# An order held by hand where attention ends and the output projection begins: weight splits among the last queries' steps, table transposes behind the first products

## The chip, the cores and the metric

The kernel runs on one core of a Trainium2 chip. The metric is device time in microseconds of one execution; the number for a kernel is the median over several executions. Five engines work side by side, each through its own queue in order: TensorE (PE, with PEld for its weight loads), VectorE (DVE), ScalarE (ACT), GpSimd (POOL) and SyncE (SP, which only issues transfers here).

## The reference, cut to what matters

One layer of a hybrid decoder on 512 prompt tokens and 8 sample tokens: two mixers, sparse attention (8 heads) and a gated recurrence (4 heads), then the output projection with a residual, then a routed mixture of 16 experts.

```python
o_nsa, o_hgrn, states = mixer(parts, l)
mixed = jnp.concatenate([rms_norm(o_nsa, g_nsa_out[l]), o_hgrn], axis=-1) @ w_out[l]
x = x + gt_a * rms_norm(mixed, g_post_mix[l])
h = rms_norm(x, g_pre_ffn[l]) * (1.0 + sc_f) + sh_f
ffn = hier_moe(h, ...)      # logits of the router: h @ w_rg, h @ w_re
x = x + gt_f * rms_norm(ffn, g_post_ffn[l])
```

## The kernel before

The program is traced in Python by generators that yield between small steps; strings such as `ORD_E` and `ORD_W` say in which order the steps are traced. A scheduler then writes the queue of each engine. It goes by the traced order among the instructions that it takes to be ready, and by its own estimate of when they are ready; so the order in a queue can differ from the traced one. `tc.issue_after(i)` adds, for each instruction that its block traces on the engine of `i`, that it stands behind `i` in that engine's queue. It adds no wait. From the routing on, the order of four engines is written out by hand; the stretch that the change touches is left to the scheduler.

**The last queries.** `attn(i)` handles 128 queries; `attn(3)` is the last (`gens["d"]`). It has eight steps (two groups of heads, four blocks of keys). A step computes scores on PE (lines 1071 and 1073, into one of two `mm` buffers), four exponentials on ACT (line 1077, into one of three `PT` buffers), and, for the first block of a group, a mask on POOL (line 1079). It then multiplies the weights of the step before by the values on PE (line 1085). After the eighth step come the last values, a square (line 1097), sums (line 1100) and the split of the result into two halves (lines 1107 and 1108). Beside it runs `hgrn_samples` (`h`), the recurrence of the eight samples: updates on DVE (line 1144), products on PE (line 1150), sums on DVE (line 1154), a norm on ACT (lines 1160, 151 and 153), a scaling on DVE (line 1162) and a transpose on PE (line 1165). The prompt's recurrence ends in transposes at line 1041.

**The splits.** A product with float32 weights is made from three products of rounded parts. `split` (lines 113 to 115) writes the high part on ACT (line 114) and the rest on DVE or POOL (line 115). `first_half` (`f`) splits the first four of eight pieces of `w_out`: loaded into `wq0` to `wq3`, high parts in `ewh0` to `ewh3`, rests in `ewr` tiles. Then it splits the four heads `mixT` of the recurrence into `mhh` and `mlh`. These tiles lie in the pool `wpa`, which is opened where the closed pools of the recurrence lay. `ORD_E` traces all four weight splits after the first step of `attn(3)`, ahead of its second.

**The projection.** `wout(hf, t, ...)` makes 24 products (line 1301) for one half of the columns and 128 tokens, first with the recurrence's parts, then with the attention's, and ACT and DVE take the result (lines 1304 and 1305). `wout_samples` does the samples (lines 1314 to 1319). `router_weights` begins by transposing the table `GC` on PE (line 1347, eight of them), and multiplies it by the router's weights (lines 1352 and 1355). `ORD_W` traces `ffhhrl...`: first product group, samples, two splits of the second half, then that part of the router. ACT also issues the transfers of `GA`, `GB` and `GC`, and the zeros for `Y` (line 1257).

Of the kernel before, what the change touches and what calls it, by code (L numbers as in the profile page):

```python
# [4 lines left out]

# [11 lines left out]
AF = mybir.ActivationFunctionType  # L17
ALU = mybir.AluOpType
# [41 lines left out]
ORD_E = "dhfdhfdhfdhfdhdhdhdhdhdhhhh"  # L60
# [6 lines left out]
def body(tc, I, O):  # L67
    nc = tc.nc
    es = ExitStack()
    dve, act, pool, pe, sp = nc.vector, nc.scalar, nc.gpsimd, nc.tensor, nc.sync  # L70
# [40 lines left out]
        return t.rearrange("p (h n) -> p h n", h=2)  # L111

    def split(src, hi, lo, eng=None):
        act.activation(hi, src, AF.Copy)  # L114
        (eng or dve).tensor_tensor(lo, src, hi.bitcast(F32), op=ALU.subtract)  # L115

    def en(i):
        return {"d": dve, "p": pool}[ENG[i]]
# [54 lines left out]
    def play(order, **gens):  # L173

        for c in order:
            next(gens[c], None)
        for g in gens.values():
            for _ in g:
                pass
# [733 lines left out]
    def gated_raw():  # L913

        with tc.issue_after(tails[3][4]):
            act.activation(hk, hl, AF.Sigmoid, scale=-1.0)
            done.append(act.activation(hl, hl, AF.Sigmoid).ins)
        for h in range(4):
            pool.tensor_scalar(hk[:, h], hk[:, h], lbt[:, 5, h:h + 1], None, op0=ALU.mult)
            dve.tensor_scalar(hsn[:, 0, h], hl[:, h, NP:T], lbt[:, 5, h:h + 1], lbt[:, 4, h:h + 1], op0=ALU.mult, op1=ALU.add)  # L920
        yield
        with tc.issue_after(tails[3][4]):
            act.activation(hq, hq, AF.Silu)
            for h in range(4):
                done.append(act.activation(mixT[4 + h], mixT[4 + h], AF.Silu).ins)
        yield
        with ExitStack() as behind:
            for i in done:
                behind.enter_context(tc.issue_after(i))
            table = act.preload_act_table_set("natural_log_exp_and_others").ins  # L930
            behind.enter_context(tc.issue_after(table))
            for h in range(4):
                act.activation(hl[:, h, 0:NP], hl[:, h, 0:NP], AF.Ln, scale=lbt[:, 5, h:h + 1], bias=lbt[:, 4, h:h + 1])
        pool.tensor_copy(hsn[:, 1], hk[:, :, NP:T])
        pool.tensor_copy(hsn[:, 2], hq[:, :, NP:T])
        for h in range(4):
            pool.tensor_copy(hsn[:, 3, h], mixT[4 + h][:, NP:T])
        yield

    def hgrn_values():  # L940
        kvs = [wip.tile([128, T], F32, name="kvt") for h in range(2)]

        def turned_values(h):
            o = kvs[h % 2]
            yield from proj_steps(22 + h, o)
            pt = ps_t()
            for t in range(4):
                pe.transpose(pt[:, 128 * t:128 * t + 128], o[:, 128 * t:128 * t + 128], ident)
            dve.tensor_copy(hv[:, :, 128 * h:128 * h + 128], pt.rearrange("p (t c) -> p t c", t=4))
            pt = ps_t()  # L950
            pe.transpose(pt[0:8, 0:128], o[:, NP:T], ident)
            dve.tensor_copy(hvs[:, 128 * h:128 * h + 128], pt[0:8, 0:128])
            yield

        yield from ahead(turned_values(h) for h in range(4))
# [90 lines left out]
    gens = dict(v=hgrn_values(), g=gated_raw(), **{"4567"[h]: mx4[h] for h in range(4)})  # L1046
# [124 lines left out]
    raw = []  # L1171
# [14 lines left out]
    hs = hgrn_samples()  # L1186
    gens.update(h=hs, o=first_weights(), w=copy_windows(), **{"abcd"[i]: attn(i) for i in range(4)})
    with contextlib.ExitStack() as order:
        if DMAN:
            order.enter_context(tc.manual_schedule(engines={pe.engine}))  # L1190
        for c in ORD_F:
            next(gens[c], None)
        drained({c: gens[c] for c in "abcow4567"})
        s_hm.close()
        s_hg.close()

        wpa = open_pool("wpa", 1, es)
        slot = [lambda dt, c=c: wpa.tile([128, D], dt, name=f"ewr{c}") for c in range(6)]  # L1200
        hslot = [lambda dt, c=c: wpa.tile([128, D], dt, name=f"ewh{c}") for c in range(4)]
        high = [h(F32R) for h in hslot]
        mh2 = [wpa.tile([128, D], F32R, name=f"mhh{c}") for c in range(4)]
        mhh, mlh = ([mh2[2 * q + h // 2][:, 512 * (h % 2):512 * (h % 2) + 512] for h in range(4)] for q in range(2))
        load_wout(slot[2](F32))
        load_wout(slot[3](F32))

        def halves(x):
            return x.rearrange("p (a b) -> p a b", a=2)

        def wout_half(hf, wh, wl):
            for q, kk in enumerate(KKS):
                c = 4 * hf + q
                lo = slot[(4, 5, 0, 1, 8, 9, 2, 3)[c]](F32R)
                split(raw[c], high[c], lo, en(93 + c))
                wh[kk], wl[kk] = halves(high[c]), halves(lo)
                yield

        ws, wt2 = ([None] * 4, [None] * 4), ([None] * 4, [None] * 4)

        def first_half():
            for _ in wout_half(0, *ws):
                pass
            yield
            for h in range(4):
                split(mixT[4 + h][:, 0:NP], mhh[h], mlh[h], en(101 + h))
                yield

        fh = first_half()
        play(ORD_E, h=hs, d=gens["d"], f=fh)  # L1230
    s_at.close()
    s_nb.close()

# [21 lines left out]
    for t in range(5):  # L1255
        n = 128 if t < 4 else 8
# [34 lines left out]
    aft = open_pool("aft", 1, s_af, "right")  # L1291
    rn = aft.tile([128, 4], F32, name="rn")

    def wout(hf, t, wh, wl):
        pm = ps_mm()
        for kk in (2, 3, 0, 1):
            for k2 in range(2):
                k = 2 * (kk % 2) + k2
                a, b = (mhi[k], mlo[k]) if kk < 2 else (mhh[k], mlh[k])
                for j, (a, b) in enumerate(((a, wh), (a, wl), (b, wh))):  # L1300
                    pe.matmul(pm[:, kk // 2], a[:, 128 * t:128 * t + 128], b[kk][:, k2],
                              start=(k == 0 and j == 0), stop=(k == 3 and j == 2))
        m = x1[t][:, 512 * hf:512 * hf + 512]
        act.activation(m, pm[:, 1], AF.Copy)
        dve.scalar_tensor_tensor(m, pm[:, 0], rn[:, t:t + 1], m, op0=ALU.mult, op1=ALU.add)
# [16 lines left out]
    GA, GB, GC = (aft.tile([128, 2, 512], F32, name=f"tab{q}") for q in range(3))  # L1322
# [9 lines left out]
    wrt = aft.tile([128, KT, 32], F32, name="wrt")  # L1332
    act.dma_start(wrt, I["wrt"])
    brt = aft.tile([128, 20], F32, name="brt")
# [5 lines left out]
    cW = aft.tile([128, 2, 20], F32, name="cW")  # L1340

    def router(src, n, w):
        hT = aft.tile([128, KT, 128], F32, name="hT", bufs=2)
        for kk in range(2):
            pt = ps_t()
            for k in range(4):
                pe.transpose(pt[:, 128 * k:128 * k + n], src[:, (4 * kk + k) * 128:(4 * kk + k + 1) * 128], ident[:n, :n])
            evac(hT[:, 4 * kk:4 * kk + 4, 0:n], pt.rearrange("p (k t) -> p k t", k=4)[:, :, 0:n])
        pl = ps_o()
        for r_ in range(2):  # L1350
            for q in range(4):
                pe.matmul(pl[32 * q:32 * q + 32, 0:n], w[:, 4 * r_ + q, :], hT[:, 4 * r_ + q, 0:n], start=(r_ == 0), stop=(r_ == 1))
        lT = aft.tile([128, 128], F32, name="lT", bufs=2)
        dve.tensor_copy(lT[:, 0:n], pl[:, 0:n])
        pe.matmul(pl[0:n, 256:276], lT[:, 0:n], sel20, start=True, stop=True)
        return pl[0:n, 256:276]
# [4 lines left out]
    mixed = {}  # L1361

    def router_weights():
        dve.tensor_tensor(cW[:, 0], router(GC.rearrange("p a b -> p (a b)"), 128, wrt), brt, op=ALU.add)
        yield
        gc = srow(aft, 0, 1, bufs=1)
        dve.tensor_tensor(cW[0:8, 1], router(gc.rearrange("p a b -> p (a b)"), 8, wrt), brt[0:8], op=ALU.add)
        yield
        for kk in range(2):
            pt = ps_t()  # L1370
            for k in range(4):
                pe.transpose(pt[:, 128 * k:128 * k + 128], GB[:, kk, 128 * k:128 * k + 128], ident)
            dve.tensor_copy(bT[:, 4 * kk:4 * kk + 4], pt.rearrange("p (k t) -> p k t", k=4)[:, :, 0])
        dve.tensor_tensor(wrb, wrt, bT.unsqueeze(2).to_broadcast([128, KT, 32]), op=ALU.mult)
# [49 lines left out]
    high = high[4:8] + mh2  # L1424
# [356 lines left out]
    last = {w: u for u, (w, c) in enumerate(units)}  # L1781
# [10 lines left out]
    with tc.manual_schedule(engines=MANUAL and {getattr(nc, e).engine for e in MANUAL}):  # L1792
# [7 lines left out]
        for o in ORD_M:  # L1800
            u = k[o] if o in k else 0
            if o in k:
                k[o] += 1
                w, c = units[min(u, len(units) - 1)]
# [65 lines left out]
    for t in range(5):  # L1870
        n = 128 if t < 4 else 8
# [18 lines left out]
    for t in (4, 0, 1):  # L1890
        n = 128 if t < 4 else 8
# [9 lines left out]
    for t in (4, 0, 1, 2, 3):  # L1901
        n = 128 if t < 4 else 8
# [3 lines left out]
    for t in (4, 0, 1, 2, 3):  # L1906
        y, yg = rows_[t]
        n = y.shape[0]
# [5 lines left out]
    for t in (4, 0, 1, 2, 3):  # L1914
        y, yg = rows_[t]
        n = y.shape[0]
# [138 lines left out]
```

## Time and profile before

| what | us |
|---|---|
| median of 3 runs | 747.39 (746.75 to 752.22) |
| the profiled execution | 741.32 |
| its span | 739.6 |
| TensorE busy in the span | 643.4 |

The page and the views give times within the span, from its start. In a timeline, equal neighbours are merged into one row (x4 is four instructions), so the busy time of a row can hold short waits between them; a bracket tells how long the engine had been idle and who ended it. [...]

### The profile page before, as it was taken

The page shows a single profiled execution, that of the slowest core. Times are in us where ns is not written, and L with a number is a line of the kernel's source. Part 1 is how long each engine was busy: PE and PEld are TensorE (multiplying, and loading weights), DVE is VectorE, ACT ScalarE, POOL GpSimd, SP SyncE. Part 2 cuts the span into 40 slices and gives each one's busy share as a digit, 9 for nine tenths or more (in the row PEclk, how much of TensorE's full clock was granted, in tenths as well). Part 3 has the DMA queues.
Part 4 walks back from the last instruction along what each step waited for, and adds up shares of the span by engine and source line. Part 5 has one row for each costly group of instructions (what it writes and reads, how often), then busy time and mean ns, then how long its engine had stood idle before and what let it go on. Part 6 is the DMA issues. An engine that isn't in the chain of part 4 may idle for free. (4 is left out here: it accounts for less than half of the span.)

```text
span 739.6 us, 13131 instructions
## 1 busy us (share of the span) xinstructions
PE 643.4 (87%) x4510; PEld 480.1 (65%) x4510; DVE 456.3 (62%) x1092; ACT 372.2 (50%) x770; POOL 153.4 (21%) x183
## 2 busy tenths in 40 slices
PE   3886898999899989899999989995889999999940
PEld 1754766779688778799776546573456677666620
DVE  3722623345686875667885254456887966888824
ACT  3322523324554545462554545346475757888833
POOL 1000310001141050150110131634211222222113
PEclk9998999999999999999999999998799999999985
DMA  8887698875554545312632274349899889998526
GB/s 282 278 292 252 219 322 294 309 260 176 184 181 143 174 125 182 118 58 85 265 119 84 92 250 140 120 136 345 279 384 356 260 230 321 346 331 287 156 31 231
DMA packets 74605, 160.83 MB, mean 217 GB/s; under 512 B 11346, under 2 KB 39538, under 8 KB 74146
## 3 DMA queue, kind: packets, MB, share of 16 engines
q1 hardware_dynamic: 59808, 125.98, 49.7%
q10 hardware_dynamic: 10690, 25.39, 10.1%
q0 software_dynamic: 4032, 8.53, 5.3%
q8 instruction: 38, 0.62, 0.4%
q14 instruction: 37, 0.30, 0.1%
HBM read 145.29 MB, written 24.28 MB: 229 GB/s over the span
## 5 line engine op out<-in xcount | busy, mean ns | idle before, releaser
L576 PE MATMUL pp<-hhi,wh 128*128 128x260 f32 x256 | 74.9, 292 | 0.3 <-ACT kvt L454 0.3
L576 PE MATMUL pp<-hlo,wh 128*128 128x260 f32 x256 | 73.1, 286 | 0.0
L576 PE MATMUL pp<-hhi,wl 128*128 128x260 f32 x256 | 72.9, 285 | 0.0
L1720 POOL DMA_INDIRECT Y<-ot,gi x17 | 24.4, 1438 | 129.9 <-ACT ot L1719 122.8
L668 ACT ACTIVATE jn<-P,M 128x128 bf16<-128x128 f32 (+3 forms) x64 | 35.9, 561 | 29.2 <-DVE M L666 24.0
L576 PEld LDWEIGHTS pp<-hhi,wh 128*128 128x128 f32 x256 | 48.2, 188 | 3.1 <-issue 2.4
L576 PEld LDWEIGHTS pp<-hlo,wh 128*128 128x128 f32 x256 | 48.2, 188 | 2.0 <-issue 1.8
L576 PEld LDWEIGHTS pp<-hhi,wl 128*128 128x128 f32 x256 | 48.2, 188 | 1.4 <-issue 1.2
L115 DVE TENSOR_TENSOR wl<-wr,wh 128x1024 fp32r<-128x1024 f32 x9 | 11.3, 1250 | 38.4 <-ACT wh L114 38.4
L1077 ACT ACTIVATE PT<-mm 128x256 f32<-128x256 f32 x80 | 24.3, 389 | 19.8 <-PE mm L1073 19.8
L666 DVE CUSTOM_DVE_ANT_0 P<-mm,tb 128x128 f32<-128x128 f32 (+3 forms) x64 | 29.1, 484 | 5.8 <-PE mm L659 5.8
L410 PE MATMUL mm<-hhi,wh 128*128 128x260 f32 x144 | 30.0, 288 | 1.3 <-ACT wh L114 1.3
L114 ACT ACTIVATE wh<-wr 128x1024 fp32r<-128x1024 f32 x9 | 9.5, 1056 | 41.7 <-PE mm L410 22.1
L410 PE MATMUL mm<-hlo,wh 128*128 128x260 f32 x144 | 30.0, 285 | 0.0
L659 PE MATMUL mm<-ka,qs 128*128 128x512 f32 (+2 forms) x112 | 27.3, 352 | 3.1 <-DVE mx L779 1.7
L1691 PE MATMUL pf<-ewi,xh 128*96 128x512 f32 x72 | 29.8, 413 | 0.0
L410 PE MATMUL mm<-hhi,wl 128*128 128x260 f32 x144 | 29.8, 287 | 0.0
L1691 PE MATMUL pf<-ewi,xl 128*96 128x512 f32 x72 | 28.8, 400 | 0.0
L1718 ACT ACTIVATE ot<-mm 96x512 f32<-96x512 f32 x17 | 10.1, 594 | 33.3 <-PE mm L1715 33.3
L1073 PE MATMUL mm<-qs,ka 128*128 128x512 f32 x80 | 25.6, 399 | 0.0
L410 PEld LDWEIGHTS mm<-hhi,wh 128*128 128x128 f32 x144 | 22.2, 188 | 5.0 <-issue 3.4
L410 PEld LDWEIGHTS mm<-hhi,wl 128*128 128x128 f32 x144 | 22.2, 188 | 3.5 <-issue 3.4
(657 smaller groups left out, 1838.6 us busy)
## 6 DMA issues: line engine op xcount, KB each, us to landing
ewr<-in_ew SPq DMA_DIRECT2D x37, 512.0 KB
wa<-in_wa SPq DMA_DIRECT2D x16, 1024.0 KB
wr<-in_wi ACTq DMA_DIRECT2D x25, 512.0 KB
ewt<-in_ew SPq DMA_DIRECT2D x24, 512.0 KB
cg<-in_cc SPq DMA_DIRECT2D x64, 128.0 KB
ewh<-in_ew SPq DMA_DIRECT2D x16, 512.0 KB
x<-in_ew SPq DMA_DIRECT2D x15, 512.0 KB
mh<-in_wa SPq DMA_DIRECT2D x13, 512.0 KB
```

Source lines behind the costliest of these rows:

```text
L114: act.activation(hi, src, AF.Copy)
L115: (eng or dve).tensor_tensor(lo, src, hi.bitcast(F32), op=ALU.subtract)
L410: pe.matmul(p[:, hf, 0:260], a[:, k, :], b[:, k, hf * 260:hf * 260 + 260], start=(k == 0 and j == 0), stop=(k == KT - 1 and j == 2))
L576: pe.matmul(p[:, 0:260], a[:, k, :], b[:, k, c], start=(k == 0 and j == 0), stop=(k == KT - 1 and j == 2))
L659: pe.matmul(o, QS[g][:, h % 4, qc], KA[g][:, j, a:b], start=(j == 0), stop=(j == 1))
L666: dve.tensor_tensor_reduce(out=p, in0=sb[:, br], in1=tb0[:, 384 - 128 * i:512].rearrange("p (k n) -> p k n", n=128), scale=SL[h], scalar=1 ...
L668: act.activation(jn[:, 0:128 * (i + 1)], p.rearrange("p k n -> p (k n)"), AF.Exp, scale=-1.0, bias=M[:, 0, i, br, h:h + 1], accum_out=M[:, ...
L1073: pe.matmul(S[:, br], KS[g][:, q, br, j], QS[g][:, :, qc], start=False, stop=(q == 1))
L1077: act.activation(PT[:, :, h], S4[:, :, h], AF.Exp, scale=-SL[4 * g + h])
L1691: pe.matmul(pg, a[:, k, :], b[:, wk_], start=(k == 0 and j == 0), stop=(k == 7 and j == 2))
L1718: act.activation(o3[:, 0], pd[:, 0], AF.Copy)
L1720: pool.indirect_dma_start(out=Y, out_offset=bass.IndirectOffsetOnAxis(ap=gix, axis=0), in_=ot, in_offset=None, bounds_check=T - 1, oob_is_ ...
```

## The change

`split` now returns its ACT instruction. `wout_half` collects them in `cuts`. While `attn(3)` is played in the order of `ORD_E`, each of its steps that is traced after the weight splits is put behind one of them in ACT's queue: the step at position 3 behind the second split, all later ones behind the fourth. In the projection, `wout` collects its last PE instruction in `wout_end`, and the PE instructions of the router's first part (eight transposes, sixteen products, two selections) are put behind the last product of the first group. No instruction is added or taken away.

```diff
     def split(src, hi, lo, eng=None):
-        act.activation(hi, src, AF.Copy)
+        cut = act.activation(hi, src, AF.Copy).ins
         (eng or dve).tensor_tensor(lo, src, hi.bitcast(F32), op=ALU.subtract)
+        return cut
...
-                split(raw[c], high[c], lo, en(93 + c))
+                cuts.append(split(raw[c], high[c], lo, en(93 + c)))
...
-        play(ORD_E, h=hs, d=gens["d"], f=fh)
+
+        last = dict(h=hs, d=gens["d"], f=fh)
+        for n, c in enumerate(ORD_E):
+            with tc.issue_after(cuts[1 if n < 6 else 3]) if cuts and c == "d" else nullcontext():
+                next(last[c], None)
+        play("", **last)
...
-                    pe.matmul(pm[:, kk // 2], a[:, 128 * t:128 * t + 128], b[kk][:, k2],
+                    mm = pe.matmul(pm[:, kk // 2], a[:, 128 * t:128 * t + 128], b[kk][:, k2],
                               start=(k == 0 and j == 0), stop=(k == 3 and j == 2))
+        wout_end.append(mm.ins)
...
-        dve.tensor_tensor(cW[:, 0], router(GC.rearrange("p a b -> p (a b)"), 128, wrt), brt, op=ALU.add)
+        with tc.issue_after(wout_end[0]):
+            dve.tensor_tensor(cW[:, 0], router(GC.rearrange("p a b -> p (a b)"), 128, wrt), brt, op=ALU.add)
```

## Rows read from the trace of the kernel before

**Rows 1.** The page's first part: busy time and share of the span of each engine.
```profile
PE 643.4 (87%) x4510; PEld 480.1 (65%) x4510; DVE 456.3 (62%) x1092; ACT 372.2 (50%) x770; POOL 153.4 (21%) x183
```

**Rows 2.** The table of stretches: the last queries, the seam, the projection, the mixture of experts. Columns: stretch, its length, busy us and instructions of PE, PEld, DVE, ACT, POOL, granted clock, DMA share, GB/s.
```profile
411.30:424.30 13.00, 13.00 (x86) 7.88 (x84) 2.18 (x8) 6.03 (x22) 1.09 (x1) 1.00 0.11 42
424.30:434.60 10.30, 7.84 (x36) 3.05 (x33) 6.97 (x9) 7.88 (x16) 5.81 (x6) 0.83 0.58 202
...
452.30:474.50 22.20, 22.18 (x143) 14.01 (x142) 13.14 (x23) 12.75 (x27) 9.37 (x7) 1.00 0.37 125
474.50:504.60 30.10, 28.10 (x166) 20.80 (x167) 13.61 (x27) 11.06 (x28) 12.55 (x8) 0.94 0.48 157
...
535.00:712.00 177.00, 166.11 (x828) 116.66 (x826) 139.78 (x198) 125.82 (x194) 38.97 (x31) 0.99 0.87 283
```

**Rows 3.** The same table, finer, inside the seam.
```profile
426.70:429.10 2.40, 0.00 (x0) 0.00 (x0) 2.40 (x4) 2.40 (x4) 0.31 (x1) 0.97 0.47 142
429.10:432.55 3.45, 3.44 (x5) 0.54 (x5) 2.78 (x4) 3.08 (x10) 3.45 (x3) 0.53 0.95 329
```

**Rows 4.** The timeline of PE from the last queries to the router's first transposes: start, busy us, line, operation, count.
```profile
409.80 0.44 PE L1041 MATMUL pt<-ident,hq 128*128 128x128 f32 x2
...
412.91 1.08 PE L1085 MATMUL po<-PT,VT 128*64 128x256 f32 x8
...
415.52 1.08 PE L1085 MATMUL po<-PT,VT 128*64 128x256 f32 x8
...
419.13 0.64 PE L1150 MATMUL pt<-S,qm 128*32 128x128 f32 x16
...
423.91 1.08 PE L1085 MATMUL po<-PT,VT 128*64 128x256 f32 x8
...
426.02 0.63 PE L1073 MATMUL mm<-qs,ka 128*128 128x512 f32 x2
429.11 1.92 PE L1314 MATMUL pf<-ewr,msn 128*32 128x512 f32 x2 [2.46 <-DVE ewr L115]
430.81 1.80 PE L1314 MATMUL pf<-ewh,msn 128*32 128x512 f32 x2
432.55 1.95 PE L1085 MATMUL po<-PT,VT 128*64 128x256 f32 x16
434.42 0.50 PE L1301 MATMUL mm<-ewh,mhh 128*128 128x512 f32 x1
...
441.11 1.08 PE L1314 MATMUL pf<-ewr,msn 128*32 128x512 f32 x8
...
444.70 1.09 PE L1347 MATMUL pt<-ident,tab 128*128 128x128 f32 x8
```

**Rows 5.** The timeline of ACT over the last queries (L1077 the exponentials, L114 the high parts, L153 the end of the samples' norm).
```profile
409.05 0.65 ACT L1077 ACTIVATE PT<-mm 128x256 f32<-128x256 f32 x2
...
415.68 1.21 ACT L1077 ACTIVATE PT<-mm 128x256 f32<-128x256 f32 x4 [1.46 <-PE mm L1073]
...
421.01 0.20 ACT L153 ACTIVATE rql<-rql 128x1 f32<-128x1 f32 x1
...
424.02 0.38 ACT L1077 ACTIVATE PT<-mm 128x256 f32<-128x256 f32 x1 [1.40 <-PE mm L1073]
424.30 3.89 ACT L114 ACTIVATE ewh<-wq 128x1024 fp32r<-128x1024 f32 x4
428.09 1.66 ACT L114 ACTIVATE mhh<-mixT 128x512 fp32r<-128x512 f32 x3
429.65 2.01 ACT L1077 ACTIVATE PT<-mm 128x256 f32<-128x256 f32 x7
```

**Rows 6.** The timeline of DVE: the last update of the samples' states, and the rests of the four weight splits.
```profile
411.66 1.40 DVE L1144 SCALAR_TENSOR_TENSOR S<-VB,hsn,S 128x128 f32<-128x128 f32 x5
...
425.57 5.70 DVE L115 TENSOR_TENSOR ewr<-wq,ewh 128x1024 fp32r<-128x1024 f32 x4
```

**Rows 7.** Behind the seam. The timeline: SP's loads, ACT's issues (ACTq) and first results, the rests of the second half's splits, PE's first product with them.
```profile
427.08 0.81 SPq L1177 DMA_DIRECT2D ewr<-in_wo  x2
427.98 0.38 SPq L1268 DMA_DIRECT2D GF<-in_ew  x1
428.56 0.33 SPq L1380 DMA_DIRECT2D xr<-in_xp  x1
...
434.62 0.39 ACTq L1325 DMA_DIRECT2D tab<-MOD  x1
435.11 6.02 ACTq L1257 DMA_DIRECT2D Y<-zero  x5
...
447.59 0.60 ACT L1304 ACTIVATE x<-mm 128x512 f32<-128x512 f32 x1 [3.92 <-issue]
...
449.65 1.23 DVE L115 TENSOR_TENSOR ewr<-ewr,ewi 128x1024 fp32r<-128x1024 f32 x1 [0.68 <-ACT ewi L114]
...
450.65 2.47 POOL L115 TENSOR_TENSOR ewr<-ewr,ewi 128x1024 fp32r<-128x1024 f32 x1 [15.43 <-ACT ewi L114]
...
452.26 0.50 PE L1301 MATMUL mm<-ewi,mhh 128*128 128x512 f32 x1
```

**Rows 8.** The table of stretches again, for the stretch in which ACT issues the zeros.
```profile
439.00:443.00 4.00, 4.00 (x29) 2.15 (x30) 0.00 (x0) 0.06 (x1) 0.00 (x0) 1.00 1.09 385
```

**Rows 9.** The list of transfers, for one of these loads: tile and source, queue, count over the whole span, size of one.
```profile
ewr<-in_wo SPq DMA_DIRECT2D x4, 512.0 KB
```

More of the change, by code (lines that the diff above doesn't have):

```diff
@@ L3 @@
 import contextlib
-from contextlib import ExitStack
+from contextlib import ExitStack, nullcontext
 import numpy as np
@@ L1209, in halves @@
             return x.rearrange("p (a b) -> p a b", a=2)
+        cuts = []
         def wout_half(hf, wh, wl):
@@ L1292, in body @@
     rn = aft.tile([128, 4], F32, name="rn")
+    wout_end = []
     def wout(hf, t, wh, wl):
```

## The prediction

> **What bounds the kernel now.** First I read the busy shares: PE has 87% of the span, the next engine 62% [rows 1]. That is an average, so next I read the table of stretches. In the last queries PE is busy for 13.00 of 13.00 us; in the seam behind them only for 7.84 of 10.30, at a mean clock of 0.83; in the projection for 22.18 of 22.20 again [rows 2]. So PE sets the end of both neighbours, and the seam is where it loses time. [...]
>
> PE's timeline gives the names [rows 4]. The scores of the eighth step end at 426.02 + 0.63 = 426.65. The next in PE's queue are four products of the samples (line 1314). The first waits 2.46 us for a rest that DVE makes; all four last until 430.81 + 1.80 = 432.61. Behind them stand the values of the last two steps, which end at 432.55 + 1.95 = 434.50. ACT's timeline gives the cause [rows 5]: after one exponential of the seventh step come four weight splits in a row (3.89 us) and three splits of heads (1.66 us); the other seven exponentials start at 429.65. DVE makes the four rests from 425.57 to 431.27 [rows 6]. Yet ACT had been idle for about 1.4 us ahead of each earlier step [rows 5]. The splits come as one lump, late. Their tiles lie where the closed pools of the recurrence lay, whose last readers are the transposes at line 1041, over at 409.80 + 0.44 = 410.24 [rows 4]. So 424.30 is an order that was written, not the first moment.
>
> **The change part by part. Splits among the steps.** Nothing is added; the work is moved. What is to be won is worked out by taking the lump away. The values of the sixth step end at 423.91 + 1.08 = 424.99, the scores of the eighth at 426.65 [rows 4]. The seventh values could follow, 0.98 us (half of the 1.95 row), to 427.63. Four exponentials (1.21 us, [rows 5]) of the eighth step run from 426.65 to 427.86, and its values from there to 428.84. The four sample products at full clock are half of a row of eight at 1.08 us: 0.54 us, to 429.38. Against 434.50 that is 5.1 us, the ceiling of this part.
>
> What the moved splits cost where they go: ACT takes 3.89 / 4 = 0.97 us for each. Begun at 410.24, two end at 412.18, and the second step's exponentials, which now end at 409.70, end at 413.39. Their values start at 412.91 now: 0.5 us late. Two more splits end at 415.33, the third step's exponentials at 416.54, and their values start at 415.52 now: 1.0 us late, not on top of the 0.5 but in its place. The head splits (1.66 us for three, about 0.6 each) fit one by one into the 1.4 us ahead of a step and cost nothing; if all three came in one gap, they would cost 0.3 us. The rests on DVE cost nothing either: DVE works for 2.18 of 13.00 us there [rows 2], and four take 5.70 [rows 6]; without that cover PE's sample products would wait for them as now. So between 4.1 us (5.1 less 1.0) and nothing is won at the last values, and I take the 4.1.
>
> **What is late next.** ACT's queue goes on with issues: a table at 434.62, then five transfers of zeros that hold it for 6.02 us, and more, so the first result of the projection is taken at 447.59, idle for 3.92 us on "issue" [rows 7]. The DMA engines are full meanwhile, at a share of 1.09 [rows 8]. SP issues its loads at 427.08, just after the last scores, which the change moves little. If ACT comes 4 us sooner, its zeros meet these loads, and what is limited by bytes does not move by 4 us. [...]
>
> PE's slack against this queue: its first product of the second half starts at 452.26, DVE's rest for it ends at 449.65 + 1.23 = 450.88, POOL's next rest at 450.65 + 2.47 = 453.12 [rows 7]. So the DVE chain has 1.38 us of room. If ACT moved by nothing, PE would lose 4.1 - 1.38 = 2.7 us again; if ACT moved by all of it, nothing. I take 1.1 us, because SP's four loads [rows 7], 512 KB each [rows 9], are 2.1 MB: at the 385 GB/s of [rows 8] they take 5.4 us from 427.08, to 432.5, and the zeros would begin at about 431: by then most of the loads are through. Net 4.1 - 1.1 = 3.0 us. Behind it the projection is PE without gaps [rows 2], and in the mixture of experts the transfers start as tiles come free, so a shift stays a shift.
>
> **Transposes behind the first products.** They run at 444.70, behind the first group and the samples' products [rows 4], already where the edge wants them. It costs and brings nothing against before: the cover is the product group. Without the edge a new order could put them ahead, where they would wait for the table issued at 434.62 [rows 7]; the edge bars that. It holds 26 PE instructions of short work and names no transfer.
>
> **The rivals.** *The samples' chain goes ahead (slower).* The scheduler wrote the splits at 424.30 though their tiles were free at 410.24: it took them to be ready late. Then the held steps are written late too, and whatever it took to be ready sooner stands ahead of the splits: the samples' norm, which ends with line 153 at 421.01 now [rows 5], is. Its last input, line 1144, ends at 411.66 + 1.40 = 413.06 [rows 6]. The chain from line 1150 at 419.13 [rows 4] to the end of line 153 at 421.21 takes 2.08 us. So the first split would start at 415.14, two end at 417.08, the second step's exponentials at 418.29: their values are 418.29 - 412.91 = 5.4 us late, and two more splits make it 5.9. That eats the ceiling of 5.1; 0.6 us of products at line 1150 are then out of the way. PE also idles from about 413 to 418, and [rows 3] show what follows idle time: 3.45 us at half speed, a loss of up to 1.6. If all four splits precede the step, it is 1.9 us more. Sum: +0.2 to +3.8 us, middle 2.0, so 749.4. It decides when the norm stands ahead of the first split in ACT's queue. For it: the late lump. Against it: that chain runs over three engines, and the trace cannot show what a new order puts where. [...]
>
> *The order does nothing.* The lump is split, but the scheduler reorders the projection so that the zeros or the loads set its start: 747.4, within 1.5 us.
>
> *More is won.* The whole 5.1 us, and the new order of the projection also takes away part of the loss in 474.50 to 504.60, where PE is idle for 30.10 - 28.10 = 2.0 us and the clock of 0.94 costs up to 1.8 [rows 2]. Together up to 8.9: 738.5 to 742, middle 741.
>
> **How the numbers follow.** The profiled execution took 741.3 us, with 1.7 us around its span, 6.1 under the median of the runs. The sum is made in it: 741.3 - 3.0 = 738.3. For the median that is 747.4 - 3.0 = 744.4 us. Chances: 0.42 for this (742.9 to 746, its own range), 0.27 for the samples' chain ahead, 0.13 for nothing, 0.18 for more. The range leaves out about a tenth at each end: 740.0, into the case of more, and 750.5, into the slower one. One per cent, 7.5 us, is about what a measurement of this kernel can tell from no change. Only the far end of "more" (a gain of 7.5 to 8.9) is faster by that: 0.10. Slower by it needs the chain ahead and a stall that no row prices: 0.05. The rest, 0.85, is within 1%.
>
> **What would show it.** In ACT's timeline the splits of line 114 should stand between the second and third steps, in two pairs, from about 410, with no lump at 424. In PE's timeline the last values should end near 430.4 instead of 434.5, the sample products without the wait of 2.46 us, and the clock of the seam should be 1.00. The transposes at line 1347 should stay behind the first group. ACT's first result should come 2 to 4 us before 447.59. I am wrong if line 1160 precedes the splits and PE idles behind 413, or if the values end early and the first product of the second half does not.

## The result and the profile after

| | before | after |
|---|---|---|
| median beside each other, us (13 runs each) | 748.52 | 752.65 |
| ratio of the times, 95% interval | | 1.0057 [1.0029, 1.0084] |
| profiled execution, us | 741.32 | 752.65 |
| its span, us | 739.6 | 750.9 |

The changed kernel is slower by 0.6%, 4.3 us. The prediction said 744.4 us, with a range of 740.0 to 750.5: the direction was wrong, and the time lies above the range.

The page's first part for the changed kernel (busy time of each engine) answers to [rows 1]; the instructions are the same, and PE's 4.5 us more go with a mean granted clock (TensorE's, as a share of full speed) of 0.949 instead of 0.958:

```profile
PE 647.9 (86%) x4510; PEld 484.5 (65%) x4510; DVE 455.1 (61%) x1092; ACT 372.2 (50%) x770; POOL 152.4 (20%) x183
```

The two profiled spans differ by 11.3 us, more than the medians do. 5.8 us of that lie ahead of the seam, where no instruction changed its place, so they are a difference between two executions. Times are therefore counted from one mark, the start of the first step's exponentials in `attn(3)` on ACT. In the kernel before, that row is the following (timeline of ACT):

```profile
405.84 1.21 ACT L1077 ACTIVATE PT<-mm 128x256 f32<-128x256 f32 x4 [1.63 <-PE mm L1073]
```

The timeline of ACT in the changed kernel (L1161 and L154 the samples' norm, L114 the high parts, L1078 the exponentials, L1265 the zeros, L1315 the projection's first result) answers to [rows 5] and [rows 7]:

```profile
411.64 1.21 ACT L1078 ACTIVATE PT<-mm 128x256 f32<-128x256 f32 x4 [1.63 <-PE mm L1074]
...
420.00 0.31 ACT L1161 ACTIVATE sq<-osn 128x128 f32<-128x128 f32 x1 [5.42 <-DVE osn L1155]
...
420.76 0.20 ACT L154 ACTIVATE rql<-rql 128x1 f32<-128x1 f32 x1
420.87 3.88 ACT L114 ACTIVATE ewh<-wq 128x1024 fp32r<-128x1024 f32 x4
424.66 1.18 ACT L1078 ACTIVATE PT<-mm 128x256 f32<-128x256 f32 x4
...
444.62 9.07 ACTq L1265 DMA_DIRECT2D Y<-zero  x5
...
460.97 0.60 ACT L1315 ACTIVATE x<-mm 128x512 f32<-128x512 f32 x1 [4.30 <-PE mm L1311]
```

The lump of four splits is still one lump. It has moved from inside the seventh step [rows 5] to ahead of the second, and the norm stands in front of it: ACT is idle for 5.42 us for the norm's input, then splits for 3.88 us, and only then come the second step's exponentials, 13.0 us behind the mark. PE's timeline shows what that costs; it answers to [rows 4] (L1086 values, L1325 samples' products):

```profile
418.89 0.64 PE L1151 MATMUL pt<-S,qm 128*32 128x128 f32 x16
421.43 0.30 PE L1166 MATMUL pt<-ident,osn 128*128 128x128 f32 x1 [1.90 <-DVE osn L1163]
425.85 1.91 PE L1325 MATMUL pf<-ewr,msn 128*32 128x512 f32 x2 [4.12 <-DVE ewr L115]
427.69 1.84 PE L1086 MATMUL po<-PT,VT 128*64 128x256 f32 x8
...
442.93 1.08 PE L1086 MATMUL po<-PT,VT 128*64 128x256 f32 x8
...
462.11 1.04 PE L1329 MATMUL pf<-sns,sel 128*32 128x512 f32 x2 [1.49 <-ACT sns L1327]
464.31 0.50 PE L1311 MATMUL mm<-ewr,mhh 128*128 128x512 f32 x1 [0.72 <-DVE ewr L115]
```

PE waits 1.90 + 4.12 = 6.02 us in the seam where it waited 2.46 before [rows 4]. The releaser that the row names is DVE's rest, since a samples' product stands ahead of the second step's values in PE's queue. The last values end at 444.01, 32.37 us behind the mark, against 434.50 - 405.84 = 28.66: 3.71 us late. Then come two waits at the second half's first products, 1.49 + 0.72 = 2.21 us together; the kernel before had none there.

The clock did as in [rows 3]. The table of stretches of the changed kernel, columns as there:

```profile
419.53:425.85 6.32, 0.31 (x2) 0.14 (x1) 4.65 (x10) 5.78 (x13) 0.00 (x0) 0.73 0.21 84
425.85:427.69 1.84, 1.84 (x2) 0.18 (x2) 1.08 (x1) 1.84 (x6) 1.25 (x1) 0.50 0.00 0
427.69:429.46 1.77, 1.77 (x9) 0.77 (x8) 0.42 (x1) 1.32 (x3) 1.77 (x3) 0.55 0.00 0
429.46:432.00 2.54, 2.54 (x16) 1.53 (x14) 0.41 (x1) 0.77 (x3) 1.56 (x1) 1.00 0.00 0
```

Behind the wait PE works for 3.6 us at a clock of 0.50 to 0.55; the kernel before had its 3.45 us at 0.53 too, so the clock hardly adds to the difference here.

SP's queue shows the second loss (timeline of SP):

```profile
441.59 0.30 SPq L1392 DMA_DIRECT2D xr<-in_xs  x1
441.98 0.81 SPq L1178 DMA_DIRECT2D ewr<-in_wo  x2
```

The loads of the second half's weights go out 30.34 us behind the mark, 21.24 before (427.08, [rows 7]). They stand behind the rows `xr`, which go out when the last scores are done. Before, the lump lay behind the last scores, so these were 7.85 us ahead of the last values' end; now there is no gap behind them, the loads start 2.0 us ahead of that end, and ACT's zeros meet them: the five issues take 9.07 us instead of 6.02 [rows 7]. ACT's first result comes 460.97 - 411.64 = 49.33 us behind the mark, 447.59 - 405.84 = 41.75 before [rows 7]: 7.58 us late, 3.87 more than the values.

### The profile page after: what moved, and what is told of

Same layout as the page of the kernel before. It is cut to its first block, busy times and chain, and to the rows that moved or that the text cites. A ratio compares the mean times of both kernels' runs of the same rounds, so it can differ in the third digit from the quotient of the medians.

```text
span 750.9 us, 13132 instructions
## 1 busy us (share of the span) xinstructions
PE 647.9 (86%) x4510; PEld 484.5 (65%) x4510; DVE 455.1 (61%) x1092; ACT 372.2 (50%) x770; POOL 152.4 (20%) x183
## 5 line engine op out<-in xcount | busy, mean ns | idle before, releaser
L1078 ACT ACTIVATE PT<-mm 128x256 f32<-128x256 f32 x80 | 24.2, 389 | 19.8 <-PE mm L1074 19.8
L114 ACT ACTIVATE wh<-wr 128x1024 fp32r<-128x1024 f32 x9 | 9.5, 1057 | 43.5 <-PE mm L411 22.0
```

What stands on the lines that cost most here:

```text
L114: cut = act.activation(hi, src, AF.Copy).ins
L1078: act.activation(PT[:, :, h], S4[:, :, h], AF.Exp, scale=-SL[4 * g + h])
```

## Experiments

Each row of the table is one profiled execution. "Values" is the last values' end less the mark, "behind" the rest of the span. The ratio is against the kernel before, run beside it.

| kernel | mark | values' end | span | values | behind | ratio, 95% |
|---|---|---|---|---|---|---|
| before | 405.84 | 434.50 | 739.6 | 28.66 | 305.1 | |
| after | 411.64 | 444.01 | 750.9 | 32.37 | 306.9 | 1.0057 [1.0029, 1.0084] |
| e10, after again | 413.19 | 445.49 | 750.9 | 32.30 | 305.4 | 1.0067 [1.0033, 1.0101] |
| e11, part 1 alone | 412.45 | 445.96 | 752.5 | 33.51 | 306.5 | 1.0102 [1.0065, 1.0139] |
| e1, norm behind | 413.40 | 444.79 | 750.7 | 31.39 | 305.9 | 1.0082 [1.0042, 1.0121] |
| e7, product behind | 407.09 | 439.58 | 744.6 | 32.49 | 305.0 | 1.0095 [1.0057, 1.0134] |
| e8, e1 and e7 | 410.31 | 435.66 | 742.0 | 25.35 | 306.3 | 0.9940 [0.9902, 0.9978] |
| e3, one split a step | 413.81 | 437.31 | 744.1 | 23.50 | 306.8 | 0.9954 [0.9914, 0.9994] |
| e12, two splits a step | 411.70 | 435.86 | 740.9 | 24.16 | 305.0 | 0.9960 [0.9929, 0.9991] |
| e4, loads ahead | 410.18 | 443.43 | 746.3 | 33.25 | 302.9 | 1.0027 [0.9991, 1.0064] |
| e9, before, loads ahead | 413.54 | 442.20 | 746.7 | 28.66 | 304.5 | 0.9967 [0.9934, 1.0000] |
| e5, e3 and e4 | 411.44 | 434.94 | 738.2 | 23.50 | 303.3 | 0.9892 [0.9852, 0.9933] |

**e1: the norm behind the splits.**
```diff
-            with tc.issue_after(cuts[1 if n < 6 else 3]) if cuts and c == "d" else nullcontext():
+            with tc.issue_after(cuts[1 if n < 6 else 3]) if cuts and c in "dh" else nullcontext():
```


> The whole computation is kept; only the steps of the samples are held behind the splits on ACT too, so that the samples' norm (line 1161) no longer stands ahead of the splits of line 114 in ACT's queue. One samples' product (line 1325) stays ahead of the second step's values in PE's queue, and SP's loads stay behind the last scores. Theory A (the loss is made in ACT's queue: norm first, then four splits, then the exponentials): in the changed kernel's trace the splits begin at 420.87 and the values of the second step at 427.69; here the splits follow line 1036 directly (413.30 + 1.28 = 414.58), end at 418.5, and the third rest of DVE, for which that product waits, ends near 419.2, so the values start near 420.5, some 7 us sooner; the kernel is 5 to 7 us below the changed one: 0.990 to 0.997 of the kernel before, middle 745.5 us. Theory B (the loss is SP's loads, which stand behind the last scores and now meet ACT's zeros): the last scores and the zeros move together, the collision stays, and no more than 2 us come back: 1.003 or more.

Measured 1.0082: theory A missed, and theory B's figure (1.003 or more) was met, though not for its reason. ACT did what was expected, PE didn't. The timeline of e1, ACT, DVE and PE:

```profile
413.40 1.21 ACT L1078 ACTIVATE PT<-mm 128x256 f32<-128x256 f32 x4 [1.63 <-PE mm L1074]
...
417.57 3.90 ACT L114 ACTIVATE ewh<-wq 128x1024 fp32r<-128x1024 f32 x4 [1.24 <-PE pt L1042]
...
421.38 1.18 ACT L1078 ACTIVATE PT<-mm 128x256 f32<-128x256 f32 x4
```
```profile
421.43 0.29 DVE L1155 TENSOR_TENSOR osn<-osn,pt 128x128 f32<-128x128 f32 x1 [0.64 <-PE pt L1151]
421.64 6.77 DVE L115 TENSOR_TENSOR ewr<-wq,ewh 128x1024 fp32r<-128x1024 f32 x4
```
```profile
426.25 1.92 PE L1325 MATMUL pf<-ewr,msn 128*32 128x512 f32 x2 [4.96 <-DVE ewr L115]
428.10 1.98 PE L1086 MATMUL po<-PT,VT 128*64 128x256 f32 x8
```

The splits begin at 417.57, released by the transposes of line 1042 (the prediction's first moment), and the exponentials end at 422.56. But PE holds the samples' product ahead of the values, until DVE's third rest; and in DVE's queue the rests stand behind line 1155, which waits for PE. The four rests also take 1.75 us each instead of 1.22 in the changed kernel, beside POOL's rests (last section). So the values start at 428.10.

**e7: the samples' products behind the first group, on PE alone.**
```diff
+                    with tc.issue_after(wout_end[0]):
                         pe.matmul(ps[32 * q:32 * q + 32], msn[:, k, :], w[kk][:, k2].bitcast(F32), start=(k < 4 and j == 0), stop=(k >= 4 and j == 1))
```


> The whole computation is kept. The changed kernel, and in PE's queue alone the samples' products (line 1325) stand behind the first product group; ACT's queue is as in the changed kernel, norm and four splits ahead of the exponentials. Theory A (ACT's queue): the second step's exponentials still end near 425.8, so its values start near 426.0 instead of 427.69: 1.5 to 2 us come back, 1.003 to 1.004 of the kernel before. Theory A' (PE's queue: the wait of 4.12 us that this product makes for DVE's rest is itself the loss): the values follow as soon as PE is free and nearly the whole 3.7 us come back: 1.001 or less. Theory B (loads): nothing, 1.005 or more.

Measured 1.0095, inside what theory B gave (1.005 or more): nothing came back. But the trace shows another reason. The first timeline row is the mark on ACT, the second PE; then the table of stretches:

```profile
407.09 1.21 ACT L1078 ACTIVATE PT<-mm 128x256 f32<-128x256 f32 x4 [1.63 <-PE mm L1074]
```
```profile
421.07 2.24 PE L1086 MATMUL po<-PT,VT 128*64 128x256 f32 x8 [3.80 <-ACT PT L1078]
```
```profile
421.07:423.20 2.13, 2.13 (x8) 1.33 (x8) 1.39 (x2) 2.13 (x7) 1.31 (x1) 0.50 0.00 0
423.20:426.00 2.80, 2.80 (x7) 1.84 (x6) 0.90 (x1) 1.26 (x3) 2.80 (x3) 0.50 0.00 0
426.00:427.60 1.60, 1.60 (x9) 0.76 (x8) 0.00 (x0) 1.21 (x4) 0.53 (x1) 0.62 0.00 0
```

Theory A's step holds: the values wait for the exponentials now, and start 13.98 us behind the mark instead of 16.05. The 2.07 us are then lost to the clock: PE works for 6.5 us at 0.50 to 0.62 instead of 3.6 us at 0.50 to 0.55, of which 1.8 lay on the product that is gone from here.

**e8: both edits.**


> The whole computation is kept. The edits of e1_norm and e7_samples together: the samples' norm behind the splits in ACT's queue, and the samples' products behind the first product group in PE's. Each alone brought nothing (1.0082 and 1.0095). Theory C: the second step's values stood behind two queues at once. In e1_norm ACT's exponentials of that step ended at 422.56, but the samples' product held PE until 428.10; in e7_samples PE was free, but the exponentials ended at 421.29, as late as in the changed kernel when both are counted from the first step. With both gone the values start about 9.2 us behind the first step's exponentials, where they stood 16.0 us behind in the changed kernel: the last values end 6 us sooner than in e1_norm, 3 us sooner than in the kernel before, and 1.7 us of that is given back at the loads: 0.997 to 1.001. Rival E (the loss is PE's lower clock behind a wait, whatever the wait): PE still waits some 1.5 us, and the clock falls all the same: 1.003 or more.

Measured 25.35 us at the values, as expected, and 0.9940, under the 0.997 to 1.001 expected: by the two columns 2.1 us are gained, by the medians 4.5, with an interval of 1.6 to 7.3. Theory C held, rival E fell. The seam's PE row:

```profile
419.26 1.35 PE L1086 MATMUL po<-PT,VT 128*64 128x256 f32 x8 [1.05 <-ACT PT L1078]
```

The lump still stands ahead of the second step, and costs PE this wait of 1.05 us; the clock over 419.26 to 422.00 is 1.00. So it was not the lump as such, which leaves e8 only 25.35 - 23.50 = 1.85 us behind e3 below: the norm in ACT's queue and the samples' product in PE's each held the second step back, and with one of them gone the other did.

**e3: one split ahead of each step.**
```diff
-            for _ in wout_half(0, *ws):
-                pass
-            yield
+            yield from wout_half(0, *ws)
...
-        for n, c in enumerate(ORD_E):
-            with tc.issue_after(cuts[1 if n < 6 else 3]) if cuts and c == "d" else nullcontext():
+        for n, c in enumerate("dhhhfdfdhfdhfdhdhffdffddd"):
+            with ExitStack() as held:
+                if n > 3:
+                    held.enter_context(tc.issue_after(tail(act)))
+                if c == "h" and n > 3:
+                    held.enter_context(tc.issue_after(tail(pe)))
```
`tail(e)` is the last instruction traced on an engine so far. The edit of e7 is in it too.

> The whole computation is kept. This is the order that the prediction took the change to write: one split ahead of each step's exponentials on ACT, the samples' norm spread behind them, the head splits in pairs ahead of the last steps, the samples' products (line 1325) behind the first product group. SP's loads stay behind the last scores. Theory A: each step's gap of 1.4 us on ACT takes one split of 0.97 us, so PE runs its steps without a gap, and the last values end 4 to 5 us sooner than in the kernel before, some 8 us sooner than in the changed one; of this 0 to 2.7 us are given back behind it: 744 to 747 us, 0.994 to 0.998 of the kernel before. Theory B: as the loads meet the zeros whatever the order of the mixing, the gain at the last values is lost again at the second half's first products: 0.999 to 1.004.

Measured 0.9954, theory A. ACT, then PE, SP's loads and the zeros' issue:

```profile
418.26 1.06 ACT L114 ACTIVATE ewh<-wq 128x1024 fp32r<-128x1024 f32 x1 [1.51 <-PE pt L1042]
419.23 1.19 ACT L1078 ACTIVATE PT<-mm 128x256 f32<-128x256 f32 x4
420.28 1.08 ACT L114 ACTIVATE ewh<-wq 128x1024 fp32r<-128x1024 f32 x1
```
```profile
436.23 1.08 PE L1086 MATMUL po<-PT,VT 128*64 128x256 f32 x8
...
455.24 1.05 PE L1335 MATMUL pf<-sns,sel 128*32 128x512 f32 x2 [1.30 <-ACT sns L1333]
457.44 0.50 PE L1316 MATMUL mm<-ewr,mhh 128*128 128x512 f32 x1 [0.73 <-DVE ewr L115]
```
```profile
435.29 0.81 SPq L1178 DMA_DIRECT2D ewr<-in_wo  x2
```
```profile
437.93 8.84 ACTq L1270 DMA_DIRECT2D Y<-zero  x5
...
454.10 0.60 ACT L1320 ACTIVATE x<-mm 128x512 f32<-128x512 f32 x1 [4.36 <-PE mm L1316]
```

PE has no wait left in the seam; the last values end 28.66 - 23.50 = 5.16 us sooner than in the kernel before. But with no gap behind the last scores the loads meet the zeros here too, and PE waits 2.03 us later on. ACT's first result comes 454.10 - 413.81 = 40.29 us behind the mark, 41.75 before: 1.46 of the 5.16 us.

**e4: SP's loads ahead of the rows.**
```diff
+    ahead_of_rows = next(i for i in reversed(nc.cur_bb.bb.instructions) if i.engine == sp.engine)
...
+        with tc.issue_after(ahead_of_rows):
             sp.dma_start(xr, I["xp"][t] if t < 4 else I["xs"])
```


> The whole computation is kept. The changed kernel, and in SP's queue alone the loads of the second half's weights (line 1178) and of GF stand ahead of the rows xr (line 1392), which wait for the last scores. Theory A: the loss is made ahead of the last values (3.7 us there); the loads bring back at most the 2.2 us that PE waits at lines 1329 and 115: 1.003 to 1.0057 of the kernel before, the mixing unchanged. Theory B: the loads start 5 us or more sooner, ACT's five issues of zeros take 6 us instead of 9.07, the first result comes 3 us sooner, and 2 to 4 us come back: 1.000 to 1.003. If the loads' own buffers come free only with the last scores, nothing moves by either theory, and it shows so in the issue times.

Measured 1.0027 [0.9991, 1.0064], 0.3% under the changed kernel beside a slower mixing (33.25, the clock again, at 0.50 to 0.54 for 5.5 us behind the wait's end): the size that theory B gave, but the interval holds theory A's range too, and so the case rests on the trace. It isn't the whole loss: the 3.7 us at the values stayed, as theory A had it. SP, DVE and ACT:

```profile
411.65 6.76 SPq L1178 DMA_DIRECT2D ewr<-in_wo  x4
```
```profile
416.18 1.40 DVE L1145 SCALAR_TENSOR_TENSOR S<-VB,hsn,S 128x128 f32<-128x128 f32 x5
```
```profile
444.05 6.65 ACTq L1265 DMA_DIRECT2D Y<-zero  x5
```

Two of the four loads go out from 1.5 us behind the mark, as in the changed kernel. The issues of the other two, which stood behind `xr`, end at 418.41, 0.83 us behind the end of DVE's line 1145 (417.58). Two issues took 0.82 us at 413.11 in the changed kernel, so these two go out from about 417.6, some 7.4 us behind the mark instead of 30.34: the rest of the delay was their place behind `xr`. The zeros go out in 6.65 us, PE's two waits are gone. The stretch behind the values is 4.0 us shorter than in the changed kernel; 2.21 of that are the waits, the rest is no more than such stretches differ by.

**e9: the same edit in the kernel before.**


> The whole computation is kept. The kernel before, and in SP's queue alone the loads of the second half's weights and of GF ahead of the rows xr, as in e4_loads. Theory C: in the kernel before the last scores ended 7.9 us ahead of the last values, so the loads had begun long before ACT's zeros, and PE did not wait at the second half's first products: nothing is to be won, 0.998 to 1.001. Theory D (an earlier load is a gain of its own): as much as in e4_loads, 0.997 or less.

Measured 0.9967 [0.9934, 1.0000]: theory D's figure, with an interval that reaches to theory C's. The profile speaks for C: the mixing is the same to the hundredth (28.66), ACT's first result comes 41.80 us behind the mark against 41.75, and the stretch behind the values is 0.6 us shorter, less than such stretches differ by (305.0 to 306.9 in the nine runs with late loads). Whether early loads help the kernel before stays open.

**e5: e3 and e4 together.**


> The whole computation is kept. Both repairs together: one split ahead of each step's exponentials (as in e3_one, which measured 0.9954), and SP's loads ahead of the rows xr (as in e4_loads, 0.3% below the changed kernel). Theory C (two separate losses, the order of the queues at the last values and the loads that meet the zeros): they add up. In e3_one the last values ended 5.2 us sooner than in the kernel before, counted from the first step's exponentials, and the stretch behind them was 1.7 us longer, with 2.0 us of waits of PE at the second half's first products; without these waits 0.9954 becomes 0.991 to 0.993, 740 to 741.5 us against 746.2. Theory D (one loss only: what the loads gave in e4_loads was the state of the clock behind the seam): 0.9945 or more.

Measured 0.9892 [0.9852, 0.9933], 739.91 against 748.07 us: theory C, a little below its 0.991 to 0.993, and a version that beats both kernels. The two savings add up: 5.16 us at the values, and a stretch of 303.3 us behind them, 3.5 us less than in e3, of which 2.03 are the waits. The timelines of SP, of PE (which has no wait between these two rows) and of ACT:

```profile
412.90 6.33 SPq L1178 DMA_DIRECT2D ewr<-in_wo  x4
```
```profile
433.86 1.08 PE L1086 MATMUL po<-PT,VT 128*64 128x256 f32 x8
...
476.19 0.66 PE L1365 MATMUL pt<-ident,tg 8*128 8x8 f32 x8 [1.50 <-POOL tg L1419]
```
```profile
448.19 0.60 ACT L1321 ACTIVATE x<-mm 128x512 f32<-128x512 f32 x1 [3.98 <-issue]
```

The first result comes 36.75 us behind the mark: with the loads out of the way 5.00 of the 5.16 us reach it.

**e12: the order that the forecast priced.** e3 with the string `dhhhffdffdhdhdhdhffdffddd`.


> The whole computation is kept. The order that the forecast of the prediction priced, two splits ahead of the second step's exponentials and two ahead of the third's, with everything else as in e3_one (one split ahead of each; there the last values ended 23.50 us behind the first step's exponentials, 28.66 us in the kernel before). The prediction's terms: the lump gone is worth 5.1 us, the two pairs cost 1.0. If both are right, the last values end some 24.5 us behind the first step's exponentials, 1.0 us later than in e3_one, and the time is 0.9965 or a little above e3_one's 0.9954. Theory F (PE works without a gap in e3_one, with some slack, so that the pairs hide too): 23.5 to 23.8 us. Theory E (each wait of PE also lowers its clock for some us): 25 us or more.

Measured 0.9960: 0.004 of 745.68 us, 3.0 us gained. At the last values 28.66 - 24.16 = 4.50 us are won; the pairs cost 0.66 against e3. PE then waits 1.72 us at the second half's first products, so the trace gives 2.8 us.

**e10 and e11: controls.** e10 is the changed kernel without an edit, e11 is it without the second part.


> The changed kernel without an edit, once more, beside these runs: 1.003 to 1.008 as before, so that the experiments can be set against it on one chip. Its trace shows whether the places named (splits in a lump behind the samples' norm, the samples' product ahead of the second step's values, loads at the last scores, zeros for some 9 us) come back with the same gaps.

> The whole computation is kept. The changed kernel without its second part: the product that makes the routing table's weights has no edge to the end of the first product group. On all five engines the instructions stand in the same order with and without that edge, so every theory expects the changed kernel's time and seam: 1.003 to 1.010 of the kernel before, the last values 32.3 us behind the first step's exponentials, the transposes behind the samples' products. Another time would mean that the edge acts by something else than the order.

e10 came back with 1.0067, 32.30 us, and the same waits of 1.90 and 4.12 us. e11 measured 1.0102; its seam has the same two waits, and its values are 1.1 us later for one reason that the stretches show: the clock stayed at 0.50 until about 432.5, 5.8 us behind the wait's end instead of 3.6. The intervals of the three runs overlap.

## Why the prediction failed

**The step that failed** is the start of the splits. The prediction took them to begin at 410.24, when their tiles come free, in two pairs between the steps. Of the 4.1 us to be won at the last values, nothing came: 3.71 were lost. The change orders the steps behind the splits; it doesn't order the splits among the steps, nor the samples' norm behind them. So the norm came first, all four splits came in one lump (420.87, which is 9.23 us behind the mark; 415.07 on the clock of the kernel before), and a second queue closed the stall: on PE the samples' product, which waits for DVE's third rest. The prediction's own rival "the samples' chain goes ahead" had this place and put the first split at 415.14. With "all four splits precede the step" (1.9 us more) its terms give 2.1 us, and 3.7 with the clock's 1.6; 3.71 were measured at the last values. It priced the end of the second step's exponentials rightly (418.29 + 1.9 = 420.2; 425.84 in the trace after, 420.04 on the clock of the kernel before). But it had no term for the samples' product, which puts the values another 1.85 us later, so that its upper end fits is in part luck. It was given 0.27; that the edges leave the splits' own order free could have been read from the diff.

**The gain's size was right for the order it assumed.** The ceiling of 5.1 us was measured as 5.16 (e3). The pairs were to win 4.1 and measured 4.50 (e12), and the whole forecast of -3.0 us is what e12 measured. That the total fits so well is in part luck: the gain was 0.4 us larger and the give-back 0.6 us larger (1.72) than forecast, and e12's interval runs from 0.7 to 5.3 us.

**The give-back was mis-sized in its cause.** The prediction wrote that SP's loads go out just after the last scores, "which the change moves little". In the order that it assumed this holds: in e3 they go out 435.29 - 413.81 = 21.48 us behind the mark, 21.24 before, and the zeros come 5.15 us sooner and meet them. That gave back 2.03 us of PE's waits, inside the bounds of nothing to 2.7, above the 1.1 taken. In the changed kernel the loads moved to 30.34 us, 3.71 with the last values and 5.4 because the gap of 7.85 us between last scores and last values closed to 2.45. Where nothing had been won, the same collision came on top of the 3.71 us with 2.21 us of waits, and the rival's sum hadn't counted it. e4 and e5 show it by taking it away. Which of the two terms carried the time over the range is not settled: 747.4 + 3.71 = 751.1 lies above it, but e4, which has the 3.71 without the waits, measured 1.0027, and that is 749.4. The prediction's working for it, what is won less what reaches ACT's first result less PE's slack of 1.38 us, gives 5.16 - 1.46 - 1.38 = 2.3 in e3, close to the 2.03; what failed is the estimate of how early the loads would be through.

The prediction's argument that the zeros meet the loads, and that what is limited by bytes does not move by 4 us, agrees in the main with e3, where 1.46 us got past the loads, and with e5, where 5.00 did once the loads were out of the way. The zeros' five issues took 8.84 us in e3 and 9.07 in the changed kernel, 2.64 us behind the loads in both; they took 6.02 in the kernel before, 8.03 us behind them, and 6.65 and 6.71 in e4 and e5, with the loads long out.

**Right:** the first moment of the splits: in e1 they start 4.17 us behind the mark, released by the transposes, where the prediction's 410.24 is 4.40. The transposes' edge is worth nothing. On every engine the order with and without it is the same, and e11 shows the changed kernel's seam. In the changed kernel no exponential passed a split (the second step's start at 424.66, behind the four splits), no value product passed the samples' product (427.69, behind 425.85), and no load passed `xr` (441.98, behind 441.59).

**Open:** why the scheduler took the norm to be ready sooner than the splits, which no run shows; and e9.

## What to carry to other kernels

An edge "B behind A" fixes two neighbours and nothing else: ask what may now stand ahead of A on that engine, and on each other engine whose result B's consumers share a queue with, for a stall with two locks gives nothing back until both are open (e1 1.0 us at the values, e7 nothing, e8 7.0). When a stall is closed, look for what its time was hiding: here a load that waited for the last scores and used the gap. A load whose buffer comes free long before belongs ahead of the one that waits, and the two repairs add up to 1.1%.

## What the runs showed of the hardware that was not expected

How long PE's clock stays near 0.50 behind the same wait differs from run to run. In the changed kernel, twice, and in e11 and e4, whose seams hold the same instructions up to the values, PE works at or near 0.50 for about 3.6, 3.6, 5.8 and 5.5 us behind the wait's end; the last values end 32.37, 32.30, 33.51 and 33.25 us behind the mark, up to 1.2 us apart. One stretch of e11, which begins 3.7 us behind the wait's end, against the row 429.46:432.00 of the changed kernel, which begins 3.6 us behind it at 1.00:

```profile
430.40:432.50 2.10, 2.10 (x7) 1.72 (x6) 0.28 (x1) 0.00 (x0) 1.42 (x1) 0.50 0.00 0
```

Rests of 128x1024 on DVE took longer where POOL made rests of 128x512 beside them. In the kernel before, DVE's first three took 1217 ns on average (window 425.50 to 428.90); the fourth began at 429.0, beside POOL's, which run from 428.79, and took 2295. The group of all four (line, form, count, busy us, mean ns, idle before), then POOL's timeline:

```profile
L115 DVE TENSOR_TENSOR ewr<-wq,ewh 128x1024 fp32r<-128x1024 f32 x4 | 5.7, 1487 | 0.0
```
```profile
428.79 5.29 POOL L115 TENSOR_TENSOR mhh<-mixT,mhh 128x512 fp32r<-128x512 f32 x3 [8.13 <-ACT mhh L114]
```

In e1 DVE's four run from 421.64 to 428.41, and POOL's three from 423.16 to 429.53. The groups again, for DVE in the changed kernel, where POOL's rests begin at 426.44, 0.5 us ahead of the end of DVE's fourth, and in e1, then for POOL in e3, where DVE is idle for most of it, and in e1:

```profile
L115 DVE TENSOR_TENSOR ewr<-wq,ewh 128x1024 fp32r<-128x1024 f32 x4 | 4.6, 1216 | 0.0
...
L115 DVE TENSOR_TENSOR ewr<-wq,ewh 128x1024 fp32r<-128x1024 f32 x4 | 6.8, 1752 | 0.0
...
L115 POOL TENSOR_TENSOR mhh<-mixT,mhh 128x512 fp32r<-128x512 f32 x3 | 3.8, 1287 | 2.1 <-ACT mhh L114 2.0
...
L115 POOL TENSOR_TENSOR mhh<-mixT,mhh 128x512 fp32r<-128x512 f32 x3 | 6.4, 2150 | 7.4 <-ACT mhh L114 7.4
```

One rest of each, one after the other, would take 1217 + 1287 = 2504 ns by these figures, an estimate; beside each other DVE's took 2295 in the kernel before, and POOL's 2150 on average in e1.
